# Seven products in another order, k and v of half the tokens first, and a later start of the weight sums

## The chip, the cores and the metric

The kernel runs on one core of a Trainium2 chip. Five engines work side by side, each through its own list of instructions in order: TensorE (PE) multiplies, VectorE (DVE) and ScalarE (ACT) do elementwise work, GpSimd (POOL) does small powers and issues some transfers, SyncE (SP) issues the transfers of weights. Times are device microseconds (us) of one execution of the whole program. "Before" is the median of three timed runs. The profile is of one more execution.

## The reference

One decoder block on 512 tokens of 1024 features: a feed-forward network (FFN1), a mixer, and a second feed-forward network (FFN2), each between two root-mean-square norms, in float32.

```python
def rms_norm(x, g):
    xf = x.astype(jnp.float32)
    y = xf * lax.rsqrt(jnp.mean(xf * xf, axis=-1, keepdims=True) + NORM_EPS)
    return (y * g.astype(jnp.float32)).astype(x.dtype)

def swiglu(x, w_gu, w_down):
    g, u = jnp.split(x @ w_gu, 2, axis=-1)
    return (jax.nn.silu(g) * u) @ w_down
...
        f = swiglu(rms_norm(h, ffn1_pre_g[l]), ffn1_w_gu[l], ffn1_w_down[l])
        h = h + MACARON_SCALE * rms_norm(f, ffn1_post_g[l])
        m = hybrid_mixer(rms_norm(h, mix_pre_g[l]), cos, sin, w_in[l], conv_w[l], conv_b[l],
                         lru_w_a[l], lru_b_a[l], lru_w_x[l], lru_b_x[l], lru_lambda[l],
                         attn_sinks[l], w_proj_lru[l], w_proj_attn[l], w_out[l])
        h = h + rms_norm(m, mix_post_g[l])
        f = swiglu(rms_norm(h, ffn2_pre_g[l]), ffn2_w_gu[l], ffn2_w_down[l])
        h = h + MACARON_SCALE * rms_norm(f, ffn2_post_g[l])
```

The mixer projects the normalised tokens with one matrix to an LRU branch x (causal convolution, block-diagonal gates, a scan), a gate branch, q, k and v for windowed attention with rotary positions, and two merge gates. The two branches are projected, merged and projected out.

## The kernel before

**Precision.** Every float32 operand of a large product is split into a high and a low part (`float32r`), and `mm3` (L145) issues three matmuls for high·high, high·low and low·high, at L146, L147 and L148. A weight comes through SP's queue into one of five raw buffers, ACT casts the high part (L116), and DVE subtracts to get the low part (L117). `wget` (L122) keeps two split weights ahead of the one in use and five raw ones, in the order of the list `worder`. Split weights, operands, residual buffers and weight sums all come from one pool of 18 large buffers (`big`).

**FFN1 and FFN2.** `gate_up` (L271) runs over 22 pairs of weight chunks, each with 24 matmuls of 128 x 512 into one of eight PSUM banks. FFN1 reads its operand from xt, the transposed input, in eight pieces that ACT scales (`u1h`, L466) and DVE splits (`u1l`, L467).

The down projection, `strassen_out` (L368), is a fast 2 x 2 block product: two halves of tokens, two halves of output features. It has seven products in the order of `PRODUCTS`, each with 66 matmuls into two banks, i = 0 and 1. Three operands for each product are cast by ACT and split by DVE in `operand` (L285, rows L292 and L293), and `combine` (L386) adds the bank to partial sums. Tokens lie in four tiles of 128. Tiles 0 and 1 take their first half of features from p2 and their second from q3, tiles 2 and 3 take both from p7. In the last product the last two weight items (three for FFN2, `TAILS`) are left until one bank can be completed after the other. The sums and differences of weight blocks that four products need come from `weight_sums` (L258): POOL's queue loads two row blocks of the down matrix (`f1tr`, 1 MB), DVE adds them four times, and POOL's queue writes the sums to device memory (`t_spill`). It starts with the first chunk, and each of its 11 steps takes four chunks.

**Boundaries.** After FFN1 comes the boundary b1: `post_norm` (L212) squares a tile on ACT with a running sum (`b1qsq`, `b1qps`), scales it by the gain on DVE (`b1rh`, L221), adds the mean (`b1qpe`, L224), has POOL take the power (`b1qpr`, L182), and adds the residual (L227). `normalise` (L191) does the same for the next norm: square on ACT, `b1nme` on DVE (L195), power on POOL, `b1un` on DVE (L197). `to_features` (L200) transposes the tile on PE in eight pieces (`b1ntp`, L206), and ACT and DVE split the result (`b1uh` L209, `b1ul` L210). b2 follows the mixer. b3 is only a post-norm, which writes the output (L230).

**What sets the order.** Work that must not stand at its first possible place is put in a generator: `start` runs it to its first `yield`, and `tick` (L135), called once for each chunk or item, counts down the number it yielded. `FEATURE_LAG` is such a number between the norm of a tile and its transposes. The framework's scheduler then orders each engine's list from this, and the engine keeps to the list.

**The mixer's start.** `x_group(0)` (L580) takes four weights and runs `first_four` (L243): four chunks on tokens 0 to 255, then the four on tokens 256 to 511, in matmuls 256 wide. Then `qkv_group(0)` computes k and v for all four tiles, `kv_tile` rotates k and, `2 + t` ticks later, transposes it; `x_group(1)` follows.

## Time and profile before

| what | us |
|---|---|
| time, median of 3 runs | 1170.25 (1169.75 to 1170.84) |
| the profiled execution, its own time | 1168.89 |
| span of its profile | 1167.1 |
| FFN1, gate and up (first matmul to p1's first) | 5.8 to 251.8 |
| FFN1, seven products (to p7's last matmul) | 251.8 to 358.7 |
| from p7's last matmul to the fourth x chunk's last | 358.7 to 397.2 |
| FFN2, seven products | 1051.3 to 1156.2 |

In rows of the timeline the first number is the start in the span, the second the duration; then the engine, the line of the kernel, the operation and output<-inputs, with buffer numbers left out. Brackets hold the engine's idle time just before and who ended it. A row with xN stands for N instructions in a run. In tables by window, each engine has its busy time and its instructions; PEclk is the TensorE clock that was granted, as a share of full speed, and the DMA share is that of 16 DMA engines. PE's matmuls overlap, so the step from one start to the next is their price: 0.227 us for 512 columns (66 matmuls in 15.0 us).

### The profile page before, as it was taken

The page shows a single profiled execution, that of the slowest core. Times are in us where ns is not written, and L with a number is a line of the kernel's source. Part 1 is how long each engine was busy: PE and PEld are TensorE (multiplying, and loading weights), DVE is VectorE, ACT ScalarE, POOL GpSimd, SP SyncE. Part 2 cuts the span into 40 slices and gives each one's busy share as a digit, 9 for nine tenths or more (in the row PEclk, how much of TensorE's full clock was granted, in tenths as well). Part 3 has the DMA queues.
Part 4 walks back from the last instruction along what each step waited for, and adds up shares of the span by engine and source line. Part 5 has one row for each costly group of instructions (what it writes and reads, how often), then busy time and mean ns, then how long its engine had stood idle before and what let it go on. Part 6 is the DMA issues. An engine that isn't in the chain of part 4 may idle for free.

```text
span 1167.1 us, 14390 instructions
## 1 busy us (share of the span) xinstructions
PE 1141.4 (98%) x5452; PEld 952.4 (82%) x5452; DVE 747.0 (64%) x1131; ACT 489.1 (42%) x760; POOL 57.7 (5%) x113
## 2 busy tenths in 40 slices
PE   8999999999997999999999999999999999999996
PEld 6888888888886988888888888888988888888885
DVE  5663465687787877997776552456533454559695
ACT  6232122246554757675465441334220231226571
POOL 1100010000001000010000000001000000100000
PEclk9999999999998999999999999999999999999998
DMA  9683383556764413122121331553645444837662
GB/s 361 244 322 113 133 274 138 178 183 196 251 209 181 144 37 127 30 98 90 37 73 58 106 128 53 180 199 129 212 167 196 181 150 156 271 136 228 222 217 109
DMA packets 61848, 190.08 MB, mean 163 GB/s; under 512 B 7249, under 2 KB 7505, under 8 KB 58961
## 3 DMA queue, kind: packets, MB, share of 16 engines
q1 hardware_dynamic: 47664, 127.79, 33.0%
q0 software_dynamic: 9504, 46.14, 10.4%
q10 hardware_dynamic: 4608, 15.21, 3.5%
q8 instruction: 43, 0.70, 0.2%
q14 instruction: 29, 0.23, 0.1%
HBM read 159.76 MB, written 29.36 MB: 162 GB/s over the span
## 4 chain that ended last, share of the span: by engine, by line
PE 66%; DVE 1%; issue 0%; POOL 0%; ACT 0%; DVEq 0%; POOLq 0%; ACTq 0%
PE f2g L148 6%; PE f2g L147 6%; PE f2g L146 6%; PE qkv L146 2%; PE qkv L147 2%; PE qkv L148 2%; PE f2p L147 2%; PE f2p L146 2%; PE f2p L148 2%; PE glg L146 1%; PE gt L146 1%; PE f2q L147 1%; PE f2q L146 1%; PE f2q L148 1%; PE glg L147 1%; PE glp L146 1%
## 5 line engine op out<-in xcount | busy, mean ns | idle before, releaser
L117 DVE TENSOR_TENSOR w<-wraw,w 128x1024 fp32r<-128x1024 f32 (+1 forms) x242 | 279.5, 1179 | 41.4 <-ACT w L116 41.3
L116 ACT CAST w<-wraw 128x1024 fp32r<-128x1024 f32 (+1 forms) x242 | 237.8, 1017 | 132.3 <-issue 35.7
L146 PE MATMUL f1g<-u1h,w 128*128 128x512 f32 x352 | 138.1, 392 | 3.2 <-ACT u1h L466 3.2
L147 PE MATMUL f1g<-u1l,w 128*128 128x512 f32 x352 | 137.9, 392 | 0.6 <-DVE u1l L467 0.6
L148 PE MATMUL f1g<-u1h,w 128*128 128x512 f32 x352 | 137.1, 391 | 0.0
L147 PE MATMUL f2g<-b2ul,w 128*128 128x512 f32 x320 | 124.5, 389 | 0.0
L146 PE MATMUL f2g<-b2uh,w 128*128 128x512 f32 x320 | 124.5, 389 | 0.0
L148 PE MATMUL f2g<-b2uh,w 128*128 128x512 f32 x320 | 124.5, 389 | 0.0
L146 PEld LDWEIGHTS f1g<-u1h,w 128*128 128x128 f32 x352 | 66.5, 189 | 17.9 <-ACT u1h L466 4.2
L147 PEld LDWEIGHTS f1g<-u1l,w 128*128 128x128 f32 x352 | 66.4, 189 | 15.5 <-DVE u1l L467 1.7
L148 PEld LDWEIGHTS f1g<-u1h,w 128*128 128x128 f32 x352 | 66.4, 189 | 13.8
L304 ACT ACTIVATE f2s<-f2g 128x512 f32<-128x512 f32 x20 | 12.0, 599 | 146.3 <-PE f2g L148 146.3
L146 PEld LDWEIGHTS f2g<-b2uh,w 128*128 128x128 f32 x320 | 60.1, 188 | 12.5
L147 PEld LDWEIGHTS f2g<-b2ul,w 128*128 128x128 f32 x320 | 60.1, 188 | 12.5
L148 PEld LDWEIGHTS f2g<-b2uh,w 128*128 128x128 f32 x320 | 60.1, 188 | 12.2
L307 ACT ACTIVATE f1s<-f1s 128x512 f32<-128x512 f32 x22 | 13.8, 632 | 128.1 <-DVE f1s L306 128.1
L309 DVE SCALAR_TENSOR_TENSOR f2p<-f2s,f2g 128x512 f32<-128x512 f32 x20 | 13.7, 686 | 59.7 <-PE f2g L148 59.6
L308 DVE SCALAR_TENSOR_TENSOR f2s<-f2s,f2g 128x512 f32<-128x512 f32 x20 | 13.7, 684 | 49.6 <-ACT f2s L304 49.6
L309 DVE SCALAR_TENSOR_TENSOR f1p<-f1s,f1g 128x512 f32<-128x512 f32 x22 | 15.1, 684 | 42.0 <-PE f1g L148 41.8
L146 PE MATMUL qkv<-w,b1uh 128*128 128x512 f32 x96 | 37.8, 395 | 0.0
L147 PE MATMUL qkv<-w,b1uh 128*128 128x512 f32 x96 | 37.7, 393 | 0.0
L148 PE MATMUL qkv<-w,b1ul 128*128 128x512 f32 x96 | 37.5, 390 | 0.0
(698 smaller groups left out, 2456.5 us busy)
## 6 DMA issues: line engine op xcount, KB each, us to landing
wraw<-in_gu_dram SPq DMA_DIRECT2D x87, 512.0 KB, 5.2
wraw<-t_spill SPq DMA_DIRECT2D x88, 256.0 KB, 4.0
wraw<-in_dn_dram SPq DMA_DIRECT2D x66, 256.0 KB, 4.2
f1tr<-in_dn_dram POOLq DMA_DIRECT2D x22, 512.0 KB, 7.4
t_spill<-f1ts POOLq DMA_DIRECT2D x11, 1024.0 KB, 6.8
f2tr<-in_dn_dram POOLq DMA_DIRECT2D x22, 512.0 KB, 5.9
t_spill<-f2ts POOLq DMA_DIRECT2D x11, 1024.0 KB, 6.5
wraw<-in_w_qkv_dram SPq DMA_DIRECT2D x12, 512.0 KB, 4.7
```

What stands on the lines that cost most here:

```text
L116: A.copy(w[:, 0, hc], raws[n][:, hc])
L117: V.tensor_tensor(out=w[:, 1, hc], in0=raws[n][:, hc], in1=w[:, 0, hc].bitcast(F32), op=ALU.subtract)
L146: PE.matmul(o, lhsT=ah, rhs=bh, start=start, stop=False)
L147: PE.matmul(o, lhsT=ah, rhs=bl, start=False, stop=False)
L148: PE.matmul(o, lhsT=al, rhs=bh, start=False, stop=stop)
L304: A.activation(s, bg, AF.Tanh, scale=0.5)
L307: A.activation(s, s, AF.Tanh, scale=0.5)
L308: V.scalar_tensor_tensor(out=s, in0=s, scalar=1.0, in1=bg, op0=ALU.add, op1=ALU.mult)
L309: V.scalar_tensor_tensor(out=ps[h][-1][:, c % 4, :], in0=s, scalar=0.5, in1=bu, op0=ALU.mult, op1=ALU.mult)
```

## The change

- `PRODUCTS` becomes p1, p6, q5, q4, p7, p2, q3. Tiles 2 and 3 are complete after p7, the fifth product; tiles 0 and 1 get their first half at p2 and their second at q3, which is now last and has the split tail. This holds for FFN1 and FFN2.
- The post-norm is a class with `part`, called for each half of a tile when it is there, and `finish`. The boundary is a class as well. Partial sums stay in their own buffers, and the residual of tiles 2 and 3 is loaded after q5.
- `FEATURE_LAG` of b1 becomes 5, 5, 4, 4.
- The mixer begins with `kv_group`: k and v of tiles 2 and 3 with four weights that are kept, then of tiles 0 and 1 with the same four. `x_group(0)` follows, in full width. The weight list has the four k and v weights first. k is transposed `KV_LAG` ticks after.
- `weight_sums` waits six chunks before its first step, and its steps take three chunks instead of four.

```diff
+KV_LAG = (3, 4, 5, 6)
+FEATURE_LAG = {"b1": (5, 5, 4, 4), "b2": (3, 3, 3, 4)}
...
-PRODUCTS = ("p1", "p6", "q5", "q4", "p2", "q3", "p7")
+PRODUCTS = ("p1", "p6", "q5", "q4", "p7", "p2", "q3")
...
-            mixer = [w_x[c] for c in range(4)] + [w_qkv[0, i] for i in range(4)]
-            mixer += [w_x[c] for c in range(4, 8)] + [w_qkv[1, i] for i in range(4)]
+            mixer = [w_qkv[0, i] for i in range(4)] + [w_x[c] for c in range(8)] + [w_qkv[1, i] for i in range(4)]
...
+    class PostNorm:
+        def __init__(self, t, g, rh, scale, name, eps):
+            self.t, self.g, self.res, self.h, self.scale, self.name, self.eps = t, g, rh[:, 0, :], rh[:, 1, :], scale, name, eps
+            self.ms2 = sm(f"{name}ps{t}", 2)
+            self.junk = t4(f"{name}sq{t}")
+            self.cols = (slice(0, 512), slice(512, 1024))
+
+        def part(self, i, src):
+            A.activation(self.junk[:, self.cols[i]], src, AF.Square, scale=1.0 / 32.0, accum_out=self.ms2[:, i:i + 1])
+            V.scalar_tensor_tensor(out=self.h[:, self.cols[i]], in0=src, scalar=self.scale, in1=self.g[:, self.cols[i]],
                                    op0=ALU.mult, op1=ALU.mult)
...
+        def finish(self, dst):
+            h, res, cols = self.h, self.res, self.cols
+            me = sm(f"{self.name}pe{self.t}")
+            V.tensor_scalar(out=me, in0=self.ms2[:, 0:1], scalar1=self.ms2[:, 1:2], scalar2=self.eps, op0=ALU.add,
+                            op1=ALU.add)
+            r = rstd(me, f"{self.name}pr{self.t}")
+            if dst is None:
+                V.scalar_tensor_tensor(out=h, in0=h, scalar=r, in1=res, op0=ALU.mult, op1=ALU.add)
+                return h
...
     def weight_sums(dn, scr, name):
+        yield 6
         for c in range(KH):
...
             G.dma_start(scr[c], ts)
-            yield 2
+            yield 1
...
+            elif prod == "p7":
+                post = epilogue.begin(2 + i)
+                V.tensor_tensor(out=keep["u", i], in0=b, in1=keep["u", i], op=ALU.add)
+                post.part(0, keep["u", i])
+                a = t2(f"{name}c{i}")
+                V.tensor_tensor(out=a, in0=keep["a", i], in1=b, op=ALU.subtract)
+                post.part(1, a)
+                start(epilogue(2 + i, post))
...
             elif prod == "p2":
-                V.tensor_tensor(out=rhs[i][:, 1, :512], in0=b, in1=keep["p1", i], op=ALU.add)
-            elif prod == "q3":
-                V.tensor_tensor(out=rhs[i][:, 1, 512:], in0=b, in1=keep["a", i], op=ALU.add)
-                start(epilogue(i, None))
+                keep["post", i] = post = epilogue.begin(i)
+                V.tensor_tensor(out=keep["p1", i], in0=b, in1=keep["p1", i], op=ALU.add)
+                post.part(0, keep["p1", i])
             else:
-                residual(2 + i)
-                V.tensor_tensor(out=rhs[2 + i][:, 1, :512], in0=b, in1=keep["u", i], op=ALU.add)
-                V.tensor_tensor(out=rhs[2 + i][:, 1, 512:], in0=keep["a", i], in1=b, op=ALU.subtract)
-                start(epilogue(2 + i, None))
...
-                if prod == "p7" and x >= len(items) - tail_n:
+                if prod == PRODUCTS[-1] and x >= len(items) - tail_n:
...
+            if prod == "q5":
+                epilogue.residual(2)
+                epilogue.residual(3)
             if prod == "q4":
-                residual(0)
-                residual(1)
+                epilogue.residual(0)
+                epilogue.residual(1)
...
-        if gi == 0:
-            first_four(u2, "x", lambda c, b: start(lru_chunk(c, b, a4, m4, bx4, c == cr[-1])))
-        else:
-            for c in cr:
-                w = wget()
-                b = bank(f"x{c}")
-                feat_chunk(b, w, u2, ALL)
-                tick()
-                start(lru_chunk(c, b, a4, m4, bx4, c == cr[-1]))
+        for c in cr:
+            w = wget()
+            b = bank(f"x{c}")
+            feat_chunk(b, w, u2, ALL)
+            tick()
+            start(lru_chunk(c, b, a4, m4, bx4, c == cr[-1]))
...
+    def kv_group():
+        ws = []
+        for tiles in ((2, 3), (0, 1)):
+            bs = {t: bank(f"kv{t}") for t in tiles}
+            for kk in range(4):
+                if len(ws) <= kk:
+                    ws.append(wget())
+                for t in tiles:
+                    qkv_block(bs[t], t, kk, ws[kk])
+                tick()
+            for t in tiles:
+                start(kv_tile(bs[t], t, kp, vt))
...
-        yield 2 + t
+        yield KV_LAG[t]
...
-    x_group(0)
-    bs = qkv_group(0)
     kp = b8("kp", [P, 2, 2, T], F32R)
     vt = b8("vt", [P, NT, NKV, 2, HD], F32R)
-    for t in range(NT):
-        start(kv_tile(bs[t], t, kp, vt))
+    kv_group()
+    x_group(0)
     x_group(1)
```

Where p2 meets q3 in FFN1, PE's list before goes straight from one product to the next. `f1p21` is p2's second bank, `f1q30` q3's first; `w73` and `w74` are weights, `f1p2s2` and `f1q3s0` operands:

```order
L146 MATMUL f1p21_2271<-w73_2332,f1p2s2_2317 128x512
L147 MATMUL f1p21_2271<-w73_2332,f1p2s2_2317 128x512
L148 MATMUL f1p21_2271<-w73_2332,f1p2s2_2317 128x512
L146 MATMUL f1q30_2384<-w74_2350,f1q3s0_2355 128x512
L147 MATMUL f1q30_2384<-w74_2350,f1q3s0_2355 128x512
L148 MATMUL f1q30_2384<-w74_2350,f1q3s0_2355 128x512
```

Now the transposes of tile 2 (`b1ntp20`, `b1ntp21`) and of tile 3 stand there:

```order
L146 MATMUL f1p21_2437<-w79_2498,f1p2s2_2483 128x512
L147 MATMUL f1p21_2437<-w79_2498,f1p2s2_2483 128x512
L148 MATMUL f1p21_2437<-w79_2498,f1p2s2_2483 128x512
L206 MATMUL b1ntp20_2516<-ident_100,b1un2_2404 128x128 x4
L206 MATMUL b1ntp21_2523<-ident_100,b1un2_2404 128x128 x4
L206 MATMUL b1ntp30_2530<-ident_100,b1un3_2427 128x128 x4
L206 MATMUL b1ntp31_2537<-ident_100,b1un3_2427 128x128 x4
L146 MATMUL f1q30_2585<-w80_2544,f1q3s0_2549 128x512
L147 MATMUL f1q30_2585<-w80_2544,f1q3s0_2549 128x512
L148 MATMUL f1q30_2585<-w80_2544,f1q3s0_2549 128x512
```

What moved: 16 transposes stand ahead of q3's first matmul, and the last eight read `b1un3`. On DVE, `b1un3` now follows the splits of weights `w80` to `w85` (q3's six) and of q3's three operands:

```order
L210 TENSOR_TENSOR b1ul1_2403<-b1ntp21_2523,b1uh1_2401 128x4x128
L117 TENSOR_TENSOR w80_2544<-wraw80_2377,w80_2544 128x1024
L298 TENSOR_TENSOR f1q3s0_2549<-f1sum0_1141,f1q3s0_2549 128x1024
L117 TENSOR_TENSOR w81_2564<-wraw81_2441,w81_2564 128x1024
L117 TENSOR_TENSOR w82_2587<-wraw82_2462,w82_2587 128x1024
L298 TENSOR_TENSOR f1q3s1_2592<-f1sum1_1430,f1q3s1_2592 128x1024
L117 TENSOR_TENSOR w83_2607<-wraw83_2480,w83_2607 128x1024
L117 TENSOR_TENSOR w84_2624<-wraw84_2501,w84_2624 128x1024
L195 TENSOR_SCALAR b1nme3_2430<-b1nms3_2428 128x1
L298 TENSOR_TENSOR f1q3s2_2629<-f1sum2_1718,f1q3s2_2629 128x768
L117 TENSOR_TENSOR w85_2644<-wraw85_2547,w85_2644 128x512
L197 SCALAR_TENSOR_TENSOR b1un3_2427<-b1rh3_2150,b1nr3_2432,g_b1_2145 128x1024
```

Before, the rows of a boundary tile (here tile 0, after q3's banks `f1q30` and `f1q31`) have no weight split between them:

```order
L401 TENSOR_TENSOR b1rh0_2264<-f1q30_2384,f1a0_2145 128x512
L401 TENSOR_TENSOR b1rh1_2266<-f1q31_2385,f1a1_2147 128x512
L221 SCALAR_TENSOR_TENSOR b1rh0_2264<-b1rh0_2264,g_b1_2261 128x512
L224 TENSOR_SCALAR b1qpe0_2502<-b1qps0_2496,eps1_111 128x1
L227 SCALAR_TENSOR_TENSOR b1rh0_2264<-b1rh0_2264,b1qpr0_2504 128x1024
L195 TENSOR_SCALAR b1nme0_2514<-b1nms0_2512 128x1
L221 SCALAR_TENSOR_TENSOR b1rh1_2266<-b1rh1_2266,g_b1_2261 128x512
L197 SCALAR_TENSOR_TENSOR b1un0_2511<-b1rh0_2264,b1nr0_2516,g_b1_2261 128x1024
```

What moved: the boundary of tiles 2 and 3 lies in the middle of the products, among their splits.

At the start of the program POOL's list before has the first loads of the weight sums (`f1tr0`) ahead of the four powers of the first norm (`n1r0` to `n1r3`):

```order
L262 DMA f1tr0_216<-in_dn1_dram 128x1024 x2
L182 TENSOR_TENSOR n1r0_185<-n1me0_182,mhalf_105 128x1
L182 TENSOR_TENSOR n1r1_194<-n1me1_191,mhalf_105 128x1
L262 DMA f1tr1_358<-in_dn1_dram 128x1024 x2
L182 TENSOR_TENSOR n1r2_203<-n1me2_200,mhalf_105 128x1
L182 TENSOR_TENSOR n1r3_212<-n1me3_209,mhalf_105 128x1
L268 DMA t_spill0_0_78<-f1ts0_286 128x2048
```

Now it has the powers first:

```order
L182 TENSOR_TENSOR n1r0_185<-n1me0_182,mhalf_105 128x1
L182 TENSOR_TENSOR n1r1_194<-n1me1_191,mhalf_105 128x1
L182 TENSOR_TENSOR n1r2_203<-n1me2_200,mhalf_105 128x1
L182 TENSOR_TENSOR n1r3_212<-n1me3_209,mhalf_105 128x1
L267 DMA f1tr0_420<-in_dn1_dram 128x1024 x2
L267 DMA f1tr1_529<-in_dn1_dram 128x1024 x2
L273 DMA t_spill0_0_78<-f1ts0_488 128x2048
```

What moved: the first two loads, 1 MB, stand behind the four powers; in the code they are six chunks later.

More of the change, by code (lines that the diff above doesn't have):

```diff
@@ L20 @@
 TAILS = (2, 7, 3)
-FEATURE_LAG = {"b1": (3, 3, 3, 3), "b2": (3, 3, 3, 4)}
+KV_LAG = (3, 4, 5, 6)
+FEATURE_LAG = {"b1": (5, 5, 4, 4), "b2": (3, 3, 3, 4)}
 ATT_GATES, ATT_Q1 = (2, 3, 4, 5, 6, 7), (0, 1)
@@ L210, in to_features @@
             V.tensor_tensor(out=ul[half][sl], in0=bv, in1=uh[half][sl].bitcast(F32), op=ALU.subtract)
-    def post_norm(banks, t, g, rh, scale, name, dst=None, eps=EPS):
-        ms2 = sm(f"{name}ps{t}", 2)
-        res, h = rh[:, 0, :], rh[:, 1, :]
-        junk = t4(f"{name}sq{t}")
-        cols = (slice(0, 512), slice(512, 1024))
-        if banks is None:
-            banks = [h[:, c] for c in cols]
-        for i in range(2):
-            A.activation(junk[:, cols[i]], banks[i], AF.Square, scale=1.0 / 32.0, accum_out=ms2[:, i:i + 1])
-            V.scalar_tensor_tensor(out=h[:, cols[i]], in0=banks[i], scalar=scale, in1=g[:, cols[i]],
-                                   op0=ALU.mult, op1=ALU.mult)
-        me = sm(f"{name}pe{t}")
-        V.tensor_scalar(out=me, in0=ms2[:, 0:1], scalar1=ms2[:, 1:2], scalar2=eps, op0=ALU.add, op1=ALU.add)
-        r = rstd(me, f"{name}pr{t}")
-        if dst is None:
-            V.scalar_tensor_tensor(out=h, in0=h, scalar=r, in1=res, op0=ALU.mult, op1=ALU.add)
-            return h
-        for i in range(2):
-            V.scalar_tensor_tensor(out=h[:, cols[i]], in0=h[:, cols[i]], scalar=r, in1=res[:, cols[i]],
-                                   op0=ALU.mult, op1=ALU.add)
-            (SP if i == 0 else A).dma_start(dst[:, cols[i]], h[:, cols[i]])
@@ new lines, in hybrid_block_kernel @@
+    class PostNorm:
[7 more added lines that the diff above has]
+            V.scalar_tensor_tensor(out=self.h[:, self.cols[i]], in0=src, scalar=self.scale, in1=self.g[:, self.cols[i]],
+                                   op0=ALU.mult, op1=ALU.mult)
+        def finish(self, dst):
[7 more added lines that the diff above has]
+                return h
+            for i in range(2):
+                V.scalar_tensor_tensor(out=h[:, cols[i]], in0=h[:, cols[i]], scalar=r, in1=res[:, cols[i]],
+                                       op0=ALU.mult, op1=ALU.add)
+                (SP if i == 0 else A).dma_start(dst[:, cols[i]], h[:, cols[i]])
@@ L364, in token_out, with strassen_out @@
                     block(t, c, w, half)
-            start(epilogue(t, (banks[t, 0], banks[t, 1])))
+            for m in range(t, min(t + 3, NT)):
+                epilogue.residual(m)
+            post = epilogue.begin(t)
+            for half in range(2):
+                post.part(half, banks[t, half])
+            start(epilogue(t, post))
             tick()
-    def strassen_out(operand, epilogue, residual, rhs, name, tail_n):
+    def strassen_out(operand, epilogue, name, tail_n):
         order = [(prod, q) for prod in PRODUCTS for q in range(3)]
@@ L397, in combine @@
                 V.tensor_tensor(out=keep["u", i], in0=b, in1=keep["u", i], op=ALU.add)
+            elif prod == "p7":
[6 more added lines that the diff above has]
+                start(epilogue(2 + i, post))
             elif prod == "p2":
-                V.tensor_tensor(out=rhs[i][:, 1, :512], in0=b, in1=keep["p1", i], op=ALU.add)
-            elif prod == "q3":
-                V.tensor_tensor(out=rhs[i][:, 1, 512:], in0=b, in1=keep["a", i], op=ALU.add)
-                start(epilogue(i, None))
-            else:
-                residual(2 + i)
-                V.tensor_tensor(out=rhs[2 + i][:, 1, :512], in0=b, in1=keep["u", i], op=ALU.add)
-                V.tensor_tensor(out=rhs[2 + i][:, 1, 512:], in0=keep["a", i], in1=b, op=ALU.subtract)
-                start(epilogue(2 + i, None))
+                keep["post", i] = post = epilogue.begin(i)
+                V.tensor_tensor(out=keep["p1", i], in0=b, in1=keep["p1", i], op=ALU.add)
+                post.part(0, keep["p1", i])
+            else:
+                post = keep["post", i]
+                V.tensor_tensor(out=keep["a", i], in0=b, in1=keep["a", i], op=ALU.add)
+                post.part(1, keep["a", i])
+                start(epilogue(i, post))
         prep(2)
@@ L432, in strassen_out, with __init__, residual, begin @@
                     tick()
-    def boundary(src, dst, gains_of, u, scale, name, eps=None):
-        rhs, g = [], []
-        def residual(t):
-            if not g:
-                g.extend(gains_of())
-            while len(rhs) < min(t + 1, NT):
-                n = len(rhs)
-                rh = b8(f"{name}rh{n}", [P, 2, D])
-                A.dma_start(rh[:, 0, :], src[n])
-                rhs.append(rh)
-        def epilogue(t, banks):
-            residual(t + 2 if banks is not None else t)
-            h = post_norm(banks, t, g[0], rhs[t], scale, f"{name}q", dst[t] if u is None else None,
-                          EPS if eps is None else eps[:, t:t + 1])
-            if u is None:
-                return
-            if not u:
-                u.extend(new_u(f"{name}u"))
-            un = normalise(h, t4(f"{name}un{t}"), t, g[1], f"{name}n")
-            A.dma_start(dst[t], h)
-            yield FEATURE_LAG[name][t]
-            to_features(un, t, u, f"{name}n")
-        return epilogue, residual, rhs
+    class Boundary:
+        def __init__(self, src, dst, gains_of, u, scale, name, eps=None):
+            self.src, self.dst, self.gains_of, self.u, self.scale, self.name, self.eps = src, dst, gains_of, u, scale, name, eps
+            self.rhs, self.g = {}, []
+        def residual(self, t):
+            if not self.g:
+                self.g.extend(self.gains_of())
+            if t not in self.rhs:
+                self.rhs[t] = b8(f"{self.name}rh{t}", [P, 2, D])
+                A.dma_start(self.rhs[t][:, 0, :], self.src[t])
+        def begin(self, t):
+            self.residual(t)
+            return PostNorm(t, self.g[0], self.rhs[t], self.scale, f"{self.name}q",
+                            EPS if self.eps is None else self.eps[:, t:t + 1])
+        def __call__(self, t, post):
+            if self.u is None:
+                post.finish(self.dst[t])
+                return
+            h = post.finish(None)
+            if not self.u:
+                self.u.extend(new_u(f"{self.name}u"))
+            un = normalise(h, t4(f"{self.name}un{t}"), t, self.g[1], f"{self.name}n")
+            A.dma_start(self.dst[t], h)
+            yield FEATURE_LAG[self.name][t]
+            to_features(un, t, self.u, f"{self.name}n")
     u1 = new_u("u1")
@@ L497, in hybrid_block_kernel @@
     hs = [dram.tile([P, D], F32, name=f"h_spill{t}") for t in range(NT)]
-    strassen_out(down1, *boundary(xv, hs, lambda: gain_pair(1, 2, "g_b1"), u2, 0.5, "b1", eps1), "f1", TAILS[0])
+    strassen_out(down1, Boundary(xv, hs, lambda: gain_pair(1, 2, "g_b1"), u2, 0.5, "b1", eps1), "f1", TAILS[0])
     vec = const.tile([P, 8, KD], F32, name="vec")
@@ L583, in x_group, with qkv_block @@
         cr = range(4 * gi, 4 * gi + 4)
-        if gi == 0:
-            first_four(u2, "x", lambda c, b: start(lru_chunk(c, b, a4, m4, bx4, c == cr[-1])))
-        else:
-            for c in cr:
-                w = wget()
-                b = bank(f"x{c}")
-                feat_chunk(b, w, u2, ALL)
-                tick()
-                start(lru_chunk(c, b, a4, m4, bx4, c == cr[-1]))
+        for c in cr:
[4 more added lines that the diff above has]
+            start(lru_chunk(c, b, a4, m4, bx4, c == cr[-1]))
+    def qkv_block(b, t, kk, w):
+        for k2 in range(2):
+            k = 2 * kk + k2
+            ns = slice(k2 * 512, (k2 + 1) * 512)
+            ts_ = slice(t * P, (t + 1) * P)
+            mm3(b, uk(u2, 0, k)[:, ts_], uk(u2, 1, k)[:, ts_], w[0][:, ns], w[1][:, ns], k == 0, k == KD - 1)
     def qkv_group(gi, unit=lambda i: None):
@@ L596, in qkv_group @@
         for kk in range(4):
-            wh, wl = wget()
+            w = wget()
             for t in range(NT):
-                for k2 in range(2):
-                    k = 2 * kk + k2
-                    ns = slice(k2 * 512, (k2 + 1) * 512)
-                    ts_ = slice(t * P, (t + 1) * P)
-                    mm3(bs[t], uk(u2, 0, k)[:, ts_], uk(u2, 1, k)[:, ts_], wh[:, ns], wl[:, ns], k == 0, k == KD - 1)
+                qkv_block(bs[t], t, kk, w)
             tick()
@@ L798, in hybrid_block_kernel @@
     hs2 = [dram.tile([P, D], F32, name=f"h2_spill{t}") for t in range(NT)]
-    epilogue, residual, _ = boundary(hs, hs2, lambda: gain_pair(3, 2, "g_b2"), u3, 1.0, "b2")
-    residual(1)
+    epilogue = Boundary(hs, hs2, lambda: gain_pair(3, 2, "g_b2"), u3, 1.0, "b2")
+    epilogue.residual(0)
+    epilogue.residual(1)
     token_out(lambda c: mg[c // 4], KD, epilogue, "wo", TAILS[1])
     down2 = gate_up(u3, "f2", dn2, scratch[1])
-    strassen_out(down2, *boundary(hs2, ov, lambda: gain_pair(5, 1, "g_b3"), None, 0.5, "b3"), "f2", TAILS[2])
+    strassen_out(down2, Boundary(hs2, ov, lambda: gain_pair(5, 1, "g_b3"), None, 0.5, "b3"), "f2", TAILS[2])
 _VECS = ["conv_b", "lru_b_a", "lru_b_x", "lru_lambda"]
```

## The prediction

> **What bounds the kernel now.** I read the page's totals first, then the list of waits, then the timeline of TensorE (PE) where the waits fall.

> ```profile
> span 1167.1 us, 14390 instructions
> PE 1141.4 (98%) x5452; PEld 952.4 (82%) x5452; DVE 747.0 (64%) x1131; ACT 489.1 (42%) x760; POOL 57.7 (5%) x113
> ...
> PE b1ntp L206 <- DVE b1un L197: 4.8, 2, 3.9
> PE x L147 <- DVE b1ul L210: 3.4, 2, 3.1
> PE f1g L146 <- ACT u1h L466: 3.2, 3, 2.5
> ```

> PE is busy for 98% of the span, so only two kinds of change count: fewer matmul microseconds, and fewer or more holes in PE. The list gives a wait as total, count and longest. Its largest rows lie at the two places that the change touches: the transposes of the boundary b1 with the first matmuls on its features, and the first chunk of FFN1.

> The seam after FFN1, in rows of start, duration, and in brackets the idle time before:

> ```profile
> 358.31 0.40 PE L148 MATMUL f1p<-w,f1p7s 128*128 128x512 f32 x1
> ...
> 362.04 0.38 PE L147 MATMUL x<-b1ul,w 128*128 128x256 f32 x1 [3.14 <-DVE b1ul L210]
> ...
> 370.40 1.97 PE L206 MATMUL b1ntp<-ident,b1un 128*128 128x128 f32 x8 [3.86 <-DVE b1un L197]
> ...
> 373.36 0.28 PE L146 MATMUL x<-b1uh,w 128*128 128x256 f32 x1
> 373.48 0.28 PE L147 MATMUL x<-b1ul,w 128*128 128x256 f32 x1
> ...
> 376.59 1.10 PE L206 MATMUL b1ntp<-ident,b1un 128*128 128x128 f32 x8 [0.91 <-DVE b1un L197]
> ...
> 397.06 0.28 PE L148 MATMUL x<-b1uh,w 128*128 128x256 f32 x1
> core 0: us, PE busy (x) PEld busy (x) DVE busy (x) ACT busy (x) POOL busy (x), PEclk, DMA share, GB/s
> 370.00:372.00 2.00, 1.60 (x8) 1.60 (x9) 1.27 (x4) 0.45 (x1) 0.55 (x1) 0.50 0.01 4
> 372.00:374.00 2.00, 2.00 (x14) 2.00 (x13) 2.00 (x3) 1.55 (x3) 0.67 (x1) 0.69 0.00 0
> ```

> The last product ends about 358.31 + 0.23 and the fourth x chunk at 397.06 + 0.12: 38.6 us. Half-width matmuls step by 0.12 (373.36 to 373.48), so 192 of them are 23.0. Two rows of eight transposes at 1.1 are 2.2, and six full-width matmuls of the LRU gates 1.4. That is 26.6 of work and **12.0 of loss**: 7.9 in the three bracketed waits, and most of the rest at a lower granted clock behind the longer ones: behind the 3.86 it was 0.50 and then 0.69, so 2 × 0.50 + 2 × 0.31 = 1.6 us were lost there.

> The trace also shows that PE does not go round a waiting instruction: it stood 3.86 us before tile 2's transposes at 370.40, and the second x chunk, on features of tokens 0 to 255 that the first had used since 362.04, came only behind them at 372.02.

> **A: a new wait between p2 and q3.** Between the last matmul of p2 and the first of q3 the new order has 16 transposes, of tiles 2 and 3. The second eight need b1un3, which stands on DVE behind five whole weight splits, a half one and the three operand splits of q3. The old order has nothing there. The durations:

> ```profile
> L146 PEld LDWEIGHTS f1p<-w,f1p1s x22: 187/188/188, 251.8 to 266.1; 128*128 128x128 f32 x22
> L146 PEld LDWEIGHTS f1p<-w,f1p6s x22: 187/188/188, 266.7 to 281.0; 128*128 128x128 f32 x22
> ...
> 326.30 0.95 DVE L293 TENSOR_TENSOR f1q3s<-f1sum,f1q3s 128x768 fp32r<-128x768 f32 x1
> 327.17 0.68 DVE L399 TENSOR_TENSOR b1rh<-f1p,f1k 128x512 f32<-128x512 f32 x1
> 327.77 0.68 DVE L117 TENSOR_TENSOR w<-wraw,w 128x512 fp32r<-128x512 f32 x1
> ...
> 328.97 1.22 DVE L117 TENSOR_TENSOR w<-wraw,w 128x1024 fp32r<-128x1024 f32 x1
> 330.10 1.22 DVE L293 TENSOR_TENSOR f1p7s<-f1p,f1p7s 128x1024 fp32r<-128x1024 f32 x1
> 331.24 1.22 DVE L117 TENSOR_TENSOR w<-wraw,w 128x1024 fp32r<-128x1024 f32 x1
> ...
> 343.38 0.27 DVE L224 TENSOR_SCALAR b1qpe<-b1qps,eps 128x1 f32<-128x1 f32 x1
> 344.33 1.28 DVE L227 SCALAR_TENSOR_TENSOR b1rh<-b1rh,b1qpr 128x1024 f32<-128x1024 f32 x1 [0.68 <-POOL b1qpr L182]
> 346.83 0.15 DVE L195 TENSOR_SCALAR b1nme<-b1nms 128x1 f32<-128x1 f32 x1 [1.22 <-ACT b1un L193]
> ...
> 353.35 0.15 DVE L195 TENSOR_SCALAR b1nme<-b1nms 128x1 f32<-128x1 f32 x1 [1.22 <-ACT b1un L193]
> 354.23 1.28 DVE L197 SCALAR_TENSOR_TENSOR b1un<-b1rh,b1nr,g_b 128x1024 f32<-128x1024 f32 x1 [0.73 <-POOL b1nr L182]
> ```

> A product takes 15.0 us of PE (251.8 to 266.7, first to first). Back to back, DVE needs 0.60 for 512 columns (327.17 to 327.77), 0.87 for 768 (326.30 to 327.17) and 1.135 for 1024 (half of 328.97 to 331.24). Count from t = 0, when p7's first bank closes.

> - DVE still has work in front; I take 1.1, from none to two wide ones (2.3). To the last scaling of tile 3 stand four combining adds, four scalings and half a split (9 × 0.60), two wide splits (2.27) and p2's last operand (0.87): 8.5, so 9.6.
> - Then the chain of tile 2, in which DVE waits for ACT and POOL: 0.95 (343.38 to 344.33), 2.50 (344.33 to 346.83), 0.88 (353.35 to 354.23), and b1un2 itself 1.2: DVE is free at 15.2. That is when p2 closes its first bank (15.0), so the next adds hardly wait.
> - Then seven rows of 512 (4.2), tile 3's residual row (1.2), two small ones (0.3), seven of 1024 (five weights and two q3 operands, 7.9), one of 768 (0.9) and b1un3 (1.3): 15.8, so **31.0**.

> PE ends p2 at 15.0 + 0.7 and tile 2's transposes near 16.4. It then waits 31.0 − 16.4 = **14.6**. The bounds follow from DVE's start: 13.5 if nothing stands ahead, 16.0 if two wide rows do. Behind the waiting transposes stand all of q3 and the mixer on PE, and for q3's matmuls wait the later weight splits, once the ready buffers are full. The cover that the change counts on, 15 us of q3, lies behind the wait and hides nothing of it.

> To this I add **1.6** for the clock behind the wait, as after the 3.86 above; 0.8 if it covers the transposes alone, 2.6 if it lasts half as long again.
> [...]

> **B: the end of FFN1.** Now q3 is last, and 24 full-width matmuls for k and v of tiles 2 and 3 cover the chain of tile 0. From q3's first bank: PE has 2.0 of q3's second bank and 24 × 0.227 = 5.4, to 7.4. b1un0 needs an add 0.60, a square of 0.73 (row below: 0.54 to its sum, and 0.19), then 0.95, 2.50, 0.88 and 1.28 as above: 6.9, so it is in time. The transposes run to 8.3. Tile 1's square of the norm stands on ACT behind the two casts of tile 0's features:

> ```profile
> 357.87 1.07 ACT L209 CAST b1uh<-b1ntp 128x512 fp32r<-128x512 f32 x2
> ...
> 360.28 0.63 ACT L220 ACTIVATE b1qsq<-b1rh 128x512 f32<-128x512 f32 x1 [1.34 <-DVE b1rh L405]
> 360.82 0.19 ACT L220 ACTIVATION_READ_ACCUMULATOR b1qsq<-b1rh 128x1 f32 x1
> ```

> The casts end near 9.0; square and mean 1.2 (1.22 in the row of 346.83), 0.88 and 1.28 give b1un1 at 12.4, a wait of 4.1. With 1.6 for the clock and 0.5 for the casts behind it, 6.2 (4 to 8) instead of 12.0: **−5.8**.
> The x chunks in full width are 96 × 0.227 = 21.8 instead of 23.0: **−1.2**.

> **C: the start.** POOL used to issue the 1 MB of the first weight sums at 1.46, among the 2 MB of xt.

> ```profile
> 1.46 1.23 POOL L262 DMA_DIRECT2D f1tr<-in_dn_dram  x2 [0.16 <-issue]
> ...
> 5.80 0.50 PE L146 MATMUL f1g<-u1h,w 128*128 128x512 f32 x1 [0.41 <-ACT u1h L466]
> ...
> 8.66 0.39 PE L148 MATMUL f1g<-u1h,w 128*128 128x512 f32 x1
> 11.59 0.80 PE L146 MATMUL f1g<-u1h,w 128*128 128x512 f32 x1 [2.53 <-ACT u1h L466]
> ...
> 17.53 0.39 PE L146 MATMUL f1g<-u1h,w 128*128 128x512 f32 x1
> ...
> 8.00:10.00 2.00, 0.78 (x3) 0.30 (x2) 0.70 (x2) 0.62 (x1) 0.00 (x0) 1.00 1.04 407
> ...
> 12.00:14.00 2.00, 2.00 (x5) 1.34 (x5) 2.00 (x4) 2.00 (x4) 0.00 (x0) 0.50 1.05 409
> ```

> The DMA engines are full (share 1.04, 407 GB/s). The first matmul starts at 5.80, and that at 17.53 opens the next chunk: 11.7 instead of 24 × 0.227 = 5.4, a loss of 6.3. Without 1 MB in front, xt lands 1.05 MB / 407 GB/s = 2.6 sooner, so the longest wait goes, and with it the half clock. Some pacing by xt's last pieces is left; I take **−4.8**, bounds 0 and −6.3.

> **D: the end of the kernel.** The last tiles now finish one half in p2, and only one add is left behind q3.

> ```profile
> 1156.23 0.69 DVE L405 TENSOR_TENSOR b3rh<-f2p,f2u 128x512 f32<-128x512 f32 x1 [0.49 <-PE f2p L148]
> ...
> 1160.89 1.41 DVE L230 SCALAR_TENSOR_TENSOR b3rh<-b3rh,b3qpr 128x512 f32<-128x512 f32 x2 [0.73 <-POOL b3qpr L182]
> ```

> From the last bank to the last scaling are 4.66 now. One add 0.60, the square 0.73, the 0.95 from the mean to the scaling and 0.5 of other DVE rows are 2.8: **−1.8** (−1 to −2.5).

> **At nothing:** the post-norm in parts has the same instructions as before. The weight sums end at chunk 39 of 44 and still lie under PE's matmuls. In FFN2, p2 has beside it 5.5 splits, three operands, four adds, four scalings and two final rows on DVE: 6.2 + 3.1 + 2.4 + 2.4 + 2.4 = 16.5 against 15.0, with no PE transposes waiting; the two weights held ready, each 12 matmuls or 2.7 of PE, cover the 1.5. Without that cover it costs 1.5. The later transposes of k lie under x chunks.

> **Sum** in the profiled execution: 14.6 + 1.6 − 5.8 − 1.2 − 4.8 − 1.8 = +2.6. It took 1168.89 us, 1.8 over its span and 1.4 under the median of the runs, 1170.25. So the forecast is **1172.9**.

> **Rivals.**
> 1. **PE is not held at tile 3's transposes** (the other side). If b1un3 comes by 16.4, A goes and the time is 1172.9 − 16.2 = 1156.7. The point is DVE: the wait must fall under 14.6 − 2.6 = 12.0 for the time not to rise, that is b1un3 must come over 2.6 earlier. For it: the five splits are not needed before q3. Against it: they stand ahead of it in DVE's order, and PE waited at 370.40 with work behind. [...] Chance 0.08.
> 2. **The delay of the weight sums frees nothing**: xt is bound by its own issue or by weights, and C is 0. The time is 1172.9 + 4.8 = 1177.7. For it: x and weights fill the same DMA engines. Against it: 407 GB/s were moved while PE waited 2.53. Chance 0.12.
> 3. **DVE's queue is shorter by some 5 us**, since ACT's and POOL's answers come while it does other rows; A is 9.6 and the time 1167.9. Against it: the chain of tile 2 is dense in the new order. Chance 0.04.

> **How the numbers follow.** The forecast has 0.76, with 1169.5 to 1177.0 as its own range from the bounds of A, B, C and D, which hardly all fall to one side. The whole range is **1168.5 to 1178.5**: it leaves out rival 1 (0.08), the upper half of rival 2 and the ends. About 0.2% (2.3 us) is what a measurement of this kernel tells from no change. Above 1172.6 lie 0.42 of the forecast's 0.76, since its range reaches further up than down, and 0.11 of rival 2; below 1167.9 lie rival 1, half of rival 3 and 0.01 of the forecast: **slower 0.53, the same 0.36, faster 0.11**.

> **What would show it.** Right: the wait for b1un on PE is 14 to 15 us in one place, just before q3's first matmul, near 338 to 352; b1un3's row follows the splits on DVE; the first chunk ends near 12 to 13; the last scaling comes 2.8 after the last bank. Wrong: no hole before q3; or the wait for u1h at the start still over 2; or a new wait for weights in q3 of FFN2.

## The result and the profile after

The changed kernel takes **1179.77 us** (median of 4 runs, 1179.01 to 1181.59) against 1170.36 before (4 runs): a ratio of 1.0083, with a 95% interval from 1.0065 to 1.0100. It is slower, as was forecast, but by 9.4 us and not by 2.6; it lies outside the range.

The profiled execution took 1181.59, the slowest of the four, and that of before 1168.89, 1.5 under its median. So the two traces are 12.7 apart, 3.3 more than the medians; in which stage that spread lies no trace tells. The working below is in traces.

The page of the changed kernel, its totals:

```profile
span 1179.8 us, 14190 instructions
...
PE 1145.7 (97%) x5356; PEld 951.0 (81%) x5356; DVE 747.2 (63%) x1131; ACT 489.3 (41%) x760; POOL 59.3 (5%) x113
```

PE has 96 instructions fewer (the wide x chunks) and yet 4 us more busy time, since a part of them ran at a lower clock (the mean granted clock is 0.985, against 0.992 before). The table by window of the changed kernel is cut at the first matmul of each stage: p2's end, q3, the first of the mixer, the first x chunk, the first gate chunk, the first merge gate, and FFN2's p1 to the end.

```profile
core 0: us, PE busy (x) PEld busy (x) DVE busy (x) ACT busy (x) POOL busy (x), PEclk, DMA share, GB/s
...
337.80:355.40 17.60, 2.65 (x18) 2.41 (x16) 17.16 (x21) 13.77 (x20) 2.28 (x2) 0.64 0.54 186
355.40:372.50 17.10, 17.10 (x68) 13.98 (x67) 3.51 (x6) 1.43 (x4) 0.00 (x0) 0.87 0.21 70
372.50:402.20 29.70, 25.62 (x114) 20.96 (x114) 21.38 (x31) 12.72 (x20) 3.85 (x8) 0.94 0.44 150
402.20:479.80 77.60, 77.60 (x346) 63.74 (x345) 59.72 (x84) 53.94 (x77) 0.00 (x0) 1.00 0.26 85
479.80:575.00 95.20, 93.15 (x481) 75.94 (x480) 79.25 (x187) 56.17 (x128) 1.31 (x6) 0.95 0.20 67
...
1065.70:1179.80 114.10, 104.93 (x463) 86.54 (x462) 85.83 (x99) 58.99 (x75) 6.86 (x4) 0.98 0.58 189
```

The same view of the kernel before, from the mixer's first matmul to the first gate chunk, from there to the first merge gate, and the end:

```profile
358.50:473.30 114.80, 106.43 (x553) 91.56 (x553) 87.75 (x125) 70.67 (x104) 4.36 (x8) 0.97 0.32 112
473.30:560.60 87.30, 87.30 (x480) 71.86 (x479) 78.50 (x186) 54.88 (x126) 4.19 (x6) 1.00 0.22 73
...
1051.30:1167.10 115.80, 104.89 (x463) 86.52 (x461) 88.97 (x104) 59.99 (x76) 3.02 (x5) 0.96 0.59 196
```

| stage, first matmul to first matmul | before | after | difference | forecast |
|---|---|---|---|---|
| start to p1 | 252.0 | 248.0 | −4.0 | −4.8 (C) |
| p1 to the mixer | 106.5 | 124.5 | +18.0 | +16.2 (A) |
| mixer to the first gate chunk | 114.8 | 107.3 | −7.5 | −7.0 (B and x) |
| first gate chunk to the first merge gate | 87.3 | 95.2 | **+7.9** | 0 |
| from there to FFN2's p1 | 490.7 | 490.7 | 0 | 0 |
| FFN2's p1 to the end | 115.8 | 114.1 | −1.7 | −1.8 (D) |
| sum | | | +12.7 | +2.6 |

Five rows out of six came near their forecast. The fourth was not in it at all: the gate stage, some 100 us behind the seam that the prediction worked out.

PE's longest waits in the changed kernel (total, count, longest), and its timeline at those places:

```profile
PE b1ntp L206 <- DVE b1un L197: 19.0, 2, 15.0
PE at000b L690 <- ACT qt L654: 1.5, 1, 1.5
```

```profile
5.62 0.50 PE L146 MATMUL f1g<-u1h,w 128*128 128x512 f32 x1
...
13.46 0.40 PE L146 MATMUL f1g<-u1h,w 128*128 128x512 f32 x1
...
337.79 1.03 PE L206 MATMUL b1ntp<-ident,b1un 128*128 128x128 f32 x8
353.78 1.97 PE L206 MATMUL b1ntp<-ident,b1un 128*128 128x128 f32 x8 [14.95 <-DVE b1un L197]
355.40 0.78 PE L146 MATMUL f1q<-w,f1q3s 128*128 128x512 f32 x1
...
359.81 0.41 PE L147 MATMUL f1q<-w,f1q3s 128*128 128x512 f32 x1
...
383.29 1.53 PE L206 MATMUL b1ntp<-ident,b1un 128*128 128x128 f32 x8 [4.07 <-DVE b1un L197]
...
387.17 0.39 PE L146 MATMUL kv<-w,b1uh 128*128 128x512 f32 x1
...
499.21 0.44 PE L690 MATMUL at000b<-kp,qt 64*128 64x128 f32 x4 [1.54 <-ACT qt L654]
500.16 0.80 PE L146 MATMUL gt<-b1uh,w 128*128 128x512 f32 x1 [0.51 <-ACT w L116]
...
510.13 0.40 PE L146 MATMUL gt<-b1uh,w 128*128 128x512 f32 x1
```

The wait between p2 and q3 stands where the order put it: PE does tile 2's eight transposes, then nothing for 14.95 us, then tile 3's eight at half speed (1.62 to the next start, against 0.85 at full clock in run 1 below), then the first of q3's matmuls at 0.43 a step, instead of 0.227, until 359.81. In the gate stage the waits are short, 1.54 and 0.51, but the clock behind them is at 0.50 until 510.04.

DVE and ACT of the changed kernel show what PE waited for (DVE first, then ACT):

```profile
336.26 1.29 DVE L197 SCALAR_TENSOR_TENSOR b1un<-b1rh,b1nr,g_b 128x1024 f32<-128x1024 f32 x1 [0.67 <-POOL b1nr L182]
...
351.31 0.68 DVE L117 TENSOR_TENSOR w<-wraw,w 128x512 fp32r<-128x512 f32 x1
352.44 1.28 DVE L197 SCALAR_TENSOR_TENSOR b1un<-b1rh,b1nr,g_b 128x1024 f32<-128x1024 f32 x1 [0.44 <-POOL b1nr L182]
...
457.10 2.33 DVE L597 TENSOR_TENSOR_SCAN lm<-la,lb 128x512 f32<-128x512 f32 x2
...
492.28 4.56 DVE L597 TENSOR_TENSOR_SCAN lm<-la,lb 128x512 f32<-128x512 f32 x4
496.76 0.66 DVE L739 SCALAR_TENSOR_TENSOR gp<-gp,gt 128x512 f32<-128x512 f32 x1
...
1171.19 0.68 DVE L422 TENSOR_TENSOR f2a<-f2q,f2a 128x512 f32<-128x512 f32 x1
...
1173.60 1.41 DVE L234 SCALAR_TENSOR_TENSOR b3rh<-b3rh,b3qpr 128x512 f32<-128x512 f32 x2 [0.73 <-POOL b3qpr L182]
```

```profile
471.75 0.62 ACT L573 CAST xch<-xc 128x512 fp32r<-128x512 f32 x1 [4.31 <-DVE xc L570]
...
497.46 0.63 ACT L740 ACTIVATE gp<-gp 128x512 f32<-128x512 f32 x1 [5.52 <-DVE gp L739]
...
498.58 0.58 ACT L654 CAST qt<-qtp 128x512 fp32r<-128x512 f32 x1
499.06 1.05 ACT L116 CAST w<-wraw 128x1024 fp32r<-128x1024 f32 x1
```

From b1un2 to b1un3 are 16.2 us of DVE, nearly without a gap; that is the first wait. The second goes back over three engines: attention's first matmul waits for the cast of q (498.58), which stands in ACT's list behind a step of the gate chain (497.46). ACT had stood 5.52 before that step for DVE's row at 496.76, which stands behind four LRU scans of 1.14 each (492.28). Before the change the scans of the first four chunks were done while x's second group ran, and the others stood in two pairs with a gate row between (DVE of the kernel before):

```profile
431.06 2.33 DVE L575 TENSOR_TENSOR_SCAN lm<-la,lb 128x512 f32<-128x512 f32 x2
433.95 2.33 DVE L575 TENSOR_TENSOR_SCAN lm<-la,lb 128x512 f32<-128x512 f32 x2
...
480.78 2.33 DVE L575 TENSOR_TENSOR_SCAN lm<-la,lb 128x512 f32<-128x512 f32 x2
483.03 0.66 DVE L704 SCALAR_TENSOR_TENSOR gp<-gp,gt 128x512 f32<-128x512 f32 x1
483.61 2.33 DVE L575 TENSOR_TENSOR_SCAN lm<-la,lb 128x512 f32<-128x512 f32 x2
```

Now the first group's scans come at 455 to 461, behind the last x chunk, where chunk 7's convolution should be: ACT waits 4.31 for it (471.75), and all that follows is later.

### The profile page after: what moved, and what is told of

It reads as the page before. It is cut to its first block, busy times and chain, and to the rows that moved or that the text cites. A ratio compares the mean times of both kernels' runs of the same rounds, so it can differ in the third digit from the quotient of the medians.

```text
span 1179.8 us, 14190 instructions
## 1 busy us (share of the span) xinstructions
PE 1145.7 (97%) x5356; PEld 951.0 (81%) x5356; DVE 747.2 (63%) x1131; ACT 489.3 (41%) x760; POOL 59.3 (5%) x113
## 4 chain that ended last, share of the span: by engine, by line
PE 92%; DVE 4%; ACT 1%; issue 1%; DMA 0%; POOL 0%; SPq 0%; ACTq 0%; DVEq 0%; POOLq 0%
PE f1g L147 7%; PE f1g L148 7%; PE f1g L146 7%; PE f2g L148 6%; PE f2g L147 6%; PE f2g L146 6%; PE f2p L147 2%; PE f2p L148 2%; PE f2p L146 2%; PE glg L146 1%; PE f1q L146 1%; PE f1q L147 1%; PE f1q L148 1%; PE qkv L146 1%; PE qkv L147 1%; PE glg L147 1%
## 5 line engine op out<-in xcount | busy, mean ns | idle before, releaser
L117 DVE TENSOR_TENSOR w<-wraw,w 128x1024 fp32r<-128x1024 f32 (+1 forms) x242 | 280.2, 1180 | 41.7 <-ACT w L116 40.8
L147 PE MATMUL f1g<-u1l,w 128*128 128x512 f32 x352 | 137.4, 390 | 0.9 <-DVE u1l L489 0.9
L146 PE MATMUL f1g<-u1h,w 128*128 128x512 f32 x352 | 137.6, 391 | 0.3 <-ACT u1h L488 0.2
L148 PE MATMUL f1g<-u1h,w 128*128 128x512 f32 x352 | 137.1, 389 | 0.0
L147 PE MATMUL f2g<-b2ul,w 128*128 128x512 f32 x320 | 124.5, 389 | 0.0
L146 PE MATMUL f2g<-b2uh,w 128*128 128x512 f32 x320 | 124.5, 389 | 0.0
L148 PE MATMUL f2g<-b2uh,w 128*128 128x512 f32 x320 | 124.5, 389 | 0.0
L147 PEld LDWEIGHTS f1g<-u1l,w 128*128 128x128 f32 x352 | 66.1, 188 | 15.5 <-DVE u1l L489 2.0
L146 PEld LDWEIGHTS f1g<-u1h,w 128*128 128x128 f32 x352 | 66.1, 188 | 15.0 <-ACT u1h L488 1.1
L148 PEld LDWEIGHTS f1g<-u1h,w 128*128 128x128 f32 x352 | 66.1, 188 | 13.6 <-DVE w L117 0.2
L147 PEld LDWEIGHTS f2g<-b2ul,w 128*128 128x128 f32 x320 | 60.1, 188 | 12.5
L146 PEld LDWEIGHTS f2g<-b2uh,w 128*128 128x128 f32 x320 | 60.1, 188 | 12.4
L148 PEld LDWEIGHTS f2g<-b2uh,w 128*128 128x128 f32 x320 | 60.1, 188 | 12.4
L311 DVE TENSOR_TENSOR f1s<-f1g,rows 128x512 f32<-128x512 f32 x22 | 15.1, 689 | 31.6 <-PE f1g L148 31.4
L146 PE MATMUL gt<-b1uh,w 128*128 128x512 f32 x64 | 27.0, 422 | 0.5 <-ACT w L116 0.5
L823 DVE SCALAR_TENSOR_TENSOR gas<-gas,gap 128x512 f32<-128x512 f32 x8 | 5.5, 688 | 32.9 <-PE gap L148 32.9
```

The lines of the kernel that those rows point to most:

```text
L117: V.tensor_tensor(out=w[:, 1, hc], in0=raws[n][:, hc], in1=w[:, 0, hc].bitcast(F32), op=ALU.subtract)
L146: PE.matmul(o, lhsT=ah, rhs=bh, start=start, stop=False)
L147: PE.matmul(o, lhsT=ah, rhs=bl, start=False, stop=False)
L148: PE.matmul(o, lhsT=al, rhs=bh, start=False, stop=stop)
L311: V.tensor_tensor(out=s, in0=bg, in1=rows, op=ALU.mult)
L823: V.scalar_tensor_tensor(out=s, in0=s, scalar=1.0, in1=b, op0=ALU.add, op1=ALU.mult)
```

## The experiments

Two theories stood against their rivals. The wait between p2 and q3 is made by PE's list alone (rival: DVE is the bound there, and q3 would wait anyway). The gate stage is late because x's eight chunks now follow each other (rival: q, or attention itself, is late).

**1. Late transposes.**

```diff
-FEATURE_LAG = {"b1": (5, 5, 4, 4), "b2": (3, 3, 3, 4)}
+FEATURE_LAG = {"b1": (5, 5, 12, 12), "b2": (3, 3, 3, 4)}
```

> The changed kernel (1179.8) with one number changed: FEATURE_LAG of b1 is (5, 5, 12, 12), so that the transposes of tiles 2 and 3 are released twelve ticks after p7 (near the end of q3) instead of four (in p2). Theory: the wait of 14.95 us between p2 and q3 and the 3.0 us of slow clock behind it come from PE's order alone. PE then goes from p2 straight into q3, the 18.0 go, and 2 to 4 us come back as shorter waits for b1un3 and its split behind q3: 1164 to 1166. The stall in the gate stage stays. Rival: DVE has more to do in p2 and q3 than PE, so q3 waits for its weight splits and operands in place of b1un3, and the time stays above 1175.

Measured: **1158.48 us** (1158.36 to 1161.36), 0.9912 of before (0.9898 to 0.9927), 21 under the changed kernel and 6 under what was expected. Its waits on PE, and the gate stage:

```profile
PE b1ntp L206 <- DVE b1un L197: 5.6, 2, 3.2
PE at000b L690 <- ACT qt L654: 1.5, 1, 1.5
...
PE gt L146 <- ACT w L116: 0.5, 1, 0.5
```

```profile
461.40:552.00 90.60, 88.55 (x482) 72.55 (x480) 79.09 (x187) 56.24 (x128) 1.32 (x6) 1.00 0.21 70
```

The 14.95 are gone and 2.4 came back in front of tile 3. DVE was not the bound: no wait is left between p2 and q3. The rest of the gain was not expected: the two waits in the gate stage are the same, 1.54 and 0.51, but the clock stays at 1.00 and the stage takes 90.6 instead of 95.2. At the seam it stays at 1.00 as well, behind a wait of 3.22. One of the four runs took 1161.36, with a mean granted clock of 0.993 instead of 0.997, so this part of the gain does not come every time.

**2. q between the two x groups.** The last four chunks' scans then stand behind the gate chunks 4 to 7 that read them, so these read values from before the scan.

```diff
-            mixer = [w_qkv[0, i] for i in range(4)] + [w_x[c] for c in range(8)] + [w_qkv[1, i] for i in range(4)]
+            mixer = [w_qkv[0, i] for i in range(4)] + [w_x[c] for c in range(4)] + [w_qkv[1, i] for i in range(4)]
+            mixer += [w_x[c] for c in range(4, 8)]
...
     x_group(0)
-    x_group(1)
...
     q0 = q_group(0)
+    x_group(1)
```

> The changed kernel with q of the first heads moved between the two groups of four x chunks (weights in the same order): k and v, x 0 to 3, q, x 4 to 7, gates. Theory: the 7.9 us lost between the first gate chunk and the merge gates come from eight x chunks in a row, whose LRU work DVE does not finish in time; the square root, the scans and the gate chain then stand late in ACT's and DVE's lists, and the cast of q that attention needs stands behind them. With q between, the waits of 1.54 and 0.51 and the slow clock behind them go: about 1172. Rival: attention waits because q itself is late or because of its narrow matmuls; then the wait for the cast of q stays and the time is within 2 us of 1179.8.

Measured: 1172.27 us, 1.0022 of before (1.0013 to 1.0031), 7.5 under the changed kernel, and no wait over 0.2 us on PE in the gate stage. Run 5 puts the scans back in order.

**3. The later weight sums alone**, on the kernel before.

```diff
     def weight_sums(dn, scr, name):
+        yield 6
...
             G.dma_start(scr[c], ts)
-            yield 2
+            yield 1
```

> The kernel before (1170.3) with only the new yields of weight_sums: six chunks before the first step, then two and one. Theory: the 1 MB of the first weight sums stands behind xt, the first chunk ends about 4.0 us sooner, nothing later waits for the sums: 1166.3. Rival: the later sums make a product wait for its weights, or the first chunk is bound by something else: 1169 or more.

Measured: 1164.41 us against 1169.59 for the runs of before beside it, 0.9957 (0.9940 to 0.9973), 1.9 under what was expected. In the trace p1's first weight load of this kernel is at 247.1, against 251.8:

```profile
L146 PEld LDWEIGHTS f1p<-w,f1p1s x22: 187/188/188, 247.1 to 261.4; 128*128 128x128 f32 x22
```

So the start is worth 4.7 by itself, and nothing later gives it back.

**4. The old order of the products in the changed kernel.** q3 then overwrites a partial sum that p7 reads, so that tiles 2 and 3 get other values.

```diff
-PRODUCTS = ("p1", "p6", "q5", "q4", "p7", "p2", "q3")
+PRODUCTS = ("p1", "p6", "q5", "q4", "p2", "q3", "p7")
...
-FEATURE_LAG = {"b1": (5, 5, 4, 4), "b2": (3, 3, 3, 4)}
+FEATURE_LAG = {"b1": (3, 3, 3, 3), "b2": (3, 3, 3, 4)}
...
-        for tiles in ((2, 3), (0, 1)):
+        for tiles in ((0, 1), (2, 3)):
```

> The changed kernel with the old order of the products (p2, q3, p7), k and v of tiles 0 and 1 first, and FEATURE_LAG of b1 at 3 throughout; the rest of the change stays. Theory: the wait between p2 and q3 goes (minus 18.0); tiles 2 and 3 are again complete at the very end, so two waits of 4 to 6 us with slow clock stand at the seam (some 8 more than now) and the end of the kernel loses its 1.7; the stall in the gate stage stays, since x still has eight chunks in a row: about 1171.5. Rival: the product order costs nothing by itself and the loss is the mixer's: near 1180.

Measured: 1169.53 us, 1.0014 of before (1.0000 to 1.0027). Its ten runs fall into two groups: six from 1168.5 to 1169.6 with a mean granted clock of 0.990 to 0.992, four from 1173.1 to 1174.5 with 0.987 or 0.988. The profiled run is one of the four. Its seam waits twice, and its gate stage is as long as that of the changed kernel:

```profile
367.91 1.94 PE L206 MATMUL b1ntp<-ident,b1un 128*128 128x128 f32 x8 [6.48 <-DVE b1un L197]
...
373.87 1.94 PE L206 MATMUL b1ntp<-ident,b1un 128*128 128x128 f32 x8 [4.02 <-DVE b1un L197]
```

```profile
354.70:393.70 39.00, 28.50 (x120) 23.26 (x121) 27.15 (x42) 15.18 (x27) 4.81 (x8) 0.82 0.45 149
...
470.80:566.10 95.30, 93.35 (x480) 76.19 (x479) 79.36 (x187) 56.02 (x127) 1.45 (x6) 0.95 0.20 67
```

The seam takes 39.0 instead of 29.7: 9.3 that the new product order saves there in this trace, for the 18 that it costs at p2. It is a trace of one of the longer runs; the six shorter ones left none, and may lose less at the seam or in the gate stage. The waits in the gate stage (1.5 and 0.4 in this trace) stand there with either order of the products.

**5. q between the x groups, with the scans in order** (as 2, and the LRU step one tick sooner).

```diff
         if not last:
             return
-        yield 2
+        yield 2 if c < 4 else 1
```

> The run with q between the x groups, with the LRU step of the second group released one tick sooner, so that each scan stands ahead of the gate chunk that reads it; the transposes of tiles 2 and 3 stand where the change put them. Theory: as there, 1171 to 1173; the wait of 15 us between p2 and q3 stays, the gate stage takes 87 to 88 us. Rival: the short gate stage there came only from gate chunks that did not wait for their scans; then waits of 2 us or more come back and it is near 1178.

Measured: 1172.75 us (1171.87 to 1173.45), 1.0028 of before (1.0016 to 1.0040). The gate stage:

```profile
477.50:566.30 88.80, 88.44 (x477) 72.03 (x476) 82.19 (x192) 67.49 (x145) 2.26 (x6) 1.00 0.25 83
```

It has 0.4 of idle PE and the full clock, with k and v still first; the 7 us are from where q stands between the x chunks. The stage is a little over the 87 to 88 expected: twelve matmuls of the LRU gates of the last x chunks now stand in it.

**6. Attention one gate chunk later**, in the changed kernel.

```diff
-ATT_GATES, ATT_Q1 = (2, 3, 4, 5, 6, 7), (0, 1)
+ATT_GATES, ATT_Q1 = (3, 4, 5, 6, 7), (0, 1, 2)
```

> The changed kernel (1179.8) with attention's first start one gate chunk later (after chunks 3 to 7 and three of q's units, not after 2 to 7 and two). Theory: ACT's list is late behind the scans and the gate chain, so PE waits all the same, 2 to 3 us, now for the cast of a weight that a gate chunk needs; the slow clock ends sooner, since full-width matmuls follow at once: 1176 to 1179. Rival: q's own chain or attention's narrow matmuls are the cause; a chunk later q is ready, nothing waits, and the time is near 1172.

Measured: 1177.66 us (1175.35 to 1179.20), 1.0070 of before (1.0055 to 1.0085). PE's waits:

```profile
PE gt L146 <- ACT w L116: 2.5, 1, 2.5
```

Attention is out of the way, and PE waits longer, now for the cast of a weight in the same list of ACT. ACT has stood the same 5.52 us for a gate row of DVE (496.23 in this trace). So the wait does not hang on q or on attention. That the low clock would end sooner can't be told: in the profiled run (1175.35) it did not fall in this stage at all (PEclk 1.00 from 478.50 to 566.70).

**7. Both edits**, 1 and 5.

> The changed kernel with both edits: FEATURE_LAG of b1 (5, 5, 12, 12) as in the run with late transposes, and q between the two groups of x chunks; the LRU step of the second group is released one tick sooner, so that each scan stands ahead of the gate chunk that reads it. Theory: the run with late transposes took 1158.5 and still had 2.05 of waits in the gate stage, with a gate stage of 90.6 against 87.3 before; with q between, those 3.3 go: 1155 to 1156, and no run above 1158, since the slow clock in the gate stage has lost its wait. Rival: the two edits meet, DVE is late again in another place: 1158 or more.

Measured: **1155.26 us** (1154.90 to 1155.83), 0.9881 of before (0.9865 to 0.9898): faster than both kernels, and as expected. Its waits at the boundary and in the gate stage, and the gate stage by window:

```profile
PE b1ntp L207 <- DVE b1un L198: 4.0, 2, 2.4
...
PE gt L149 <- DVE w L118: 0.4, 1, 0.4
```

```profile
459.90:548.60 88.70, 88.33 (x477) 71.97 (x475) 82.11 (x192) 67.41 (x145) 2.28 (x6) 1.00 0.25 84
```

## Why the prediction was right and wrong

**The sign, and A's mechanism, were right.** The wait stood before tile 3's transposes, 14.95 us against the 14.6 worked out, and DVE's list was as dense as counted. Run 1 shows that PE's order alone made it: with the transposes later, 15 us of q3 cover the same DVE work.

**The step that failed** is the line of x in B and the paragraph "At nothing". The mixer's new order was priced by PE alone: a width (−1.2) and "the later transposes of k lie under x chunks". Eight x chunks in a row move LRU work on DVE, scans of 1.14 us each among it, from behind the first four chunks to behind the last. No row of a scan was quoted and no term spoke of it. The runs show +7.9 in its place: 2.05 of waits, 4.6 of low clock (95.2 against the 90.6 of run 1, which has the same waits at full clock), and 1.2 in attention's first matmuls (run 1 has 88.55 busy there at full clock, against 87.30 before). These are the same matmuls as before, but on PE they now stand in pieces of 4, 8, 6 and 6 instead of 12 and 12. Of the 10.1 us between the sum and the traces this stage is 7.9, A is 1.8 and C 0.8. Runs 2 and 5 take the waits and the low clock away by the order of the mixer (PEclk 1.00 in run 5; in run 2 no matmul of a gate chunk takes over 0.51, against 0.80 at 500.16 above), run 6 leaves a wait of 2.5 when attention moves, and run 4 leaves waits and low clock when the products move.

**A's clock was too small**: 1.6 forecast, with a bound of 2.6; 3.0 measured (0.8 in the transposes, and q3 took 17.1 instead of 15.0). The row it was read from had a wait of 3.86 behind it, not of 15, and the 1.6 also counts 0.4 of idle time in that row as work at half clock. By its own terms A's upper bound is 15.8, not 16.0; nothing hangs on that.

**B** was right with x: −7.5 for −7.0. One wait of 4.07 was left, for 4.1 worked out.

**C** was mis-sized a little: −4.0 for −4.8. The first chunk went from 11.7 to 7.8 (5.62 to 13.46), not to 6.9. Run 3 gives 4.7 alone. In the eight traces with the later sums p1's first weight load lies between 247.0 and 248.1, so that most of the difference is spread between executions.

**D** was right: from the last add to the last scaling 2.4 us (1171.19 to 1173.60), for 2.8, and −1.7 in the stage.

**The rivals:** none of them came. Rival 1, PE not held, was the version that run 1 builds by another release number: 1158.5 against its 1156.7. That they lie so close is in part luck: against rival 1's sum, run 1 has 2.4 of wait in front of tile 3 and 3.3 more in the gate stage, and about 2.5 less at the seam, where the clock stayed full. The range failed because it was made of bounds for the terms that were counted, and had no room for a stage that was not.

What stays open: why the scheduler set four scans ahead of the gate row, when before it set two and two, was not tried apart from the mixer's order. No run moved a wait on purpose to see when the clock falls; what the last section says of it is read from the traces of the two kernels and of runs 1 and 7.

## What to carry to other kernels

When blocks of matmuls change places, list for each what follows it on every other engine, and see in the new order where that work lands; here PE's own sum (−1.2) was the smaller part (+7.9 came back). A release number that fits the time at which data could be ready does not fit a queue in which 15 us of other work stand ahead: release PE's work on it after that queue has drained. And price a short wait with its clock behind it: here the clock behind 2.05 us of waits cost nothing in run 1 and 4.6 us, more than twice the waits, in the changed kernel.
